# Scoring one head group in whole fp32 on small array tiles, in a two-layer attention encoder on one Trainium2 core

## The chip, the cores and the metric

The kernel runs on one core of a Trainium2 chip. A core has five engines that run side by side and meet at semaphores: TensorE (PE: matrix products, with its weight loads shown as PEld), VectorE (DVE), ScalarE (ACT), GpSimd (POOL) and SyncE (SP, which issues the transfers). Products land in PSUM, in eight banks of 512 fp32 columns; everything else that is computed on lies in SBUF, with 128 partitions. The metric is the time of one execution on the device in microseconds (us), as the median of several runs.

## The reference

The model is an encoder block of two layers on 512 tokens of width 1024, with 16 heads of 64. The change touches layer A, whose mixer has three groups of heads that differ in dilation (1, 4 and 16), each with its own queries, keys and values; the groups are merged by their softmax denominators.

```python
def mixer_a(hn, w_in, w_out, q_gain, k_gain, t5_bias):
    proj = hn @ w_in
    ...
    for g, (window, dilation) in enumerate(DILATED_PAIRS):     # (128,1), (512,4), (2048,16)
        q = rms_norm(qkv[:, :, g, 0], q_gain[g])
        k = rms_norm(qkv[:, :, g, 1], k_gain[g])
        v = qkv[:, :, g, 2]
        reach = (window // 2) // dilation
        o, lse = dilated_group_attention(q, k, v, t5_bias[...], dilation, reach)
    ...
    alpha = jax.nn.softmax(jnp.stack(lses), axis=0)
    y = jnp.sum(alpha[..., None] * jnp.stack(outs), axis=0)
    y = y.reshape(b, s, BRANCH_WIDTH).astype(hn.dtype) * jax.nn.silu(gate)
    return y @ w_out
```

Each query of group 0 sees the 64 tokens on either side; the logits are q.k/8 plus a bias by distance, all in float32. Layer B is a neighbourhood attention on an 8 x 64 grid, built alike: norm, one projection, per-head norm of queries and keys, softmax, gate, output projection.

## The kernel before

**Tiles and passes.** The 16 heads go through as eight pairs (`hc` 0 to 7), each pair filling 128 partitions, one head in the lower 64 and one in the upper. For most products float32 values are split in two halves, a rounded high part `h` and the rest `l`, both of type fp32r, and a product is made of three: h.h, h.l and l.h (`mm3`, L221). Weights come in by SyncE into `wraw`, ScalarE rounds them to `wh` (L132), and VectorE or GpSimd subtracts to give `wl` (L138). The projections are the bulk of TensorE's work (tile `acc`).

**Order of the work.** TensorE's order is written out by hand. A main generator yields after each group of projection products; a side generator makes the attention, and `run` (L932) lets the side go on whenever a clock of the kernel's own (`clock`, L209, advanced by an estimate of each product in `matmul`, L211) passes the time at which the side's next piece is due. The due times are delays in ns of that clock after stamps such as `("rawk", hc + 1)`. The other engines' instructions are ordered when the program is built, some of them pinned by `keep_in_program_order`.

**Queries and keys of layer A.** Of each pair the projection gives `rawq` with four column blocks of 128: queries of groups 0, 1 and 2, and keys of group 0. For pairs 0 to 5 (`moved`, L446) VectorE transposes 32x32 blocks in place (L571), and the tile goes to DRAM and back (`move_q`, L609: one write, four reads) into `qt`, which has four slots: slots 0 to 2 the queries of groups 0 to 2, slot 3 the keys of group 0, now with a head's 64 dimensions on the partitions. For pairs 6 and 7, `q_a` (L587) transposes on TensorE instead (`transpose4`) and copies out of PSUM. Group 0's queries and keys are then split: `split_q` (L639) or `q_a` fill `q0h`, `q0l`, `k0h`, `k0l`, with the product of the query and key gains (`gk`) folded into one of the two by `put_k` (L658). The keys of groups 1 and 2 lie in `k12` in plain float32, transposed and scaled in `k_a` (L560).

**Scores.** `scores(u)` in `attn_a` (L789, L797) makes the logits of two tiles of 128 queries, t = 2u and 2u+1, for both heads, each tile and head in a PSUM bank `log`: columns 0 to 255 for group 0 (a window of 192 or 256 keys), columns 256 to 511 for the dilated groups. Group 0 goes first for both tiles, by `mm3_heads` (L226): three split products for each head, of 64 rows (the head's dimensions) by 128 columns (queries) of the array, the two heads in its two halves. Then come groups 1 and 2: for each group g, each j of 4 slices of 32 queries and each head, one product in plain float32 on an array tile of 64 rows by 32 columns:

```python
matmul(
    lgs[hd][32 * j : 32 * j + 32, 256 + P * g : 384 + P * g],
    qt[hs, t, 1 + g, 32 * j : 32 * j + 32],
    k12[hs, g, P * j : P * j + P],
    share=2, start=False, stop=(g == 1),
)
```

So slice j meets keys 128j to 128j+127 of its own residue class. VectorE adds the bias and finds the minimum of the negated logits (L835, L846), ScalarE takes the exponential (L857), and later `weigh` makes the weighted sums `o`.

**Layer B.** `side_b` (L1050) splits its queries and keys in the same way into tiles `qh`, `ql`, `kh`, `kl`, which use the same four buffers (the tags `q0h`, `q0l`, `k0h`, `k0l`), and scores with `mm3_heads`.

Of the kernel before, what the change touches and what calls it, by code (L numbers as in the profile page):

```python
# [22 lines left out]
P = 128  # L23
S = 512
# [7 lines left out]
EXT = S + 64  # L32
# [14 lines left out]
def tile_hybrid_encoder(  # L47
# [12 lines left out]
    nc = tc.nc  # L60
# [5 lines left out]
    wk = ctx.enter_context(tc.tile_pool(name="wk", bufs=2))  # L66
# [19 lines left out]
    def bank(name):  # L86

        return ps_side.tile([P, 512], F32, tag="side", name=name)
# [122 lines left out]
    def matmul(o, l, r, share=1, **kw):  # L211

        cols = max(r.free_size() / 2.4, l.free_size() / 1.2)
        clock[0] += (cols if r.dtype == F32R else r.free_size() * 4 / 2.4 * l.free_size() / P) / share
        nc.tensor.matmul(o, l, r, **kw)  # L215
# [166 lines left out]
    gk = cp.tile([P, 4], F32, name="gk")  # L382
# [59 lines left out]
    st = {}  # L442
# [133 lines left out]
    def q_tiles():  # L576


        return (
            wk.tile([P, 512], F32R, tag="q0h", name="q0h", bufs=1),  # L580
            wk.tile([P, 512], F32R, tag="q0l", name="q0l", bufs=1),
            wk.tile([P, 4, 4, P], F32, tag="q12", name="qt", bufs=1),
            wk.tile([P, EXT], F32R, tag="k0h", name="k0h", bufs=1),
            wk.tile([P, EXT], F32R, tag="k0l", name="k0l", bufs=1),
        )

    def q_a(hc):  # L587

        yield "wait", ("rawq", hc), 18000 if moved(hc) else 13000 if hc < NHC - 1 else 23500
        raw = st.pop(("rawq", hc))  # L590
        if moved(hc):
            move_q(hc, raw)
            return
        st["q", hc] = q0h, q0l, qt, k0h, k0l = q_tiles()

        tp = transpose4(raw, 0)
        nc.scalar.copy(tjr(q0h), to_tjr(tp))
        nc.vector.tensor_sub(tjr(q0l), to_tjr(tp), tjr(q0h.bitcast(F32)))
        yield
        tp = transpose4(raw, 3 * P)  # L600
        put_k([(trj(k0h[:, 64:EXT]), trj(k0l[:, 64:EXT]), to_trj(tp))], 0)
        yield
        for g in range(2):
            tp = transpose4(raw, (g + 1) * P)
            nc.vector.tensor_copy(qt[:, :, 1 + g, :].rearrange("p t (j r) -> p t j r", j=4), to_tjr(tp))
            yield
        stamp["q", hc] = 0

    def move_q(hc, raw):  # L609

        d = dr.tile([4, P, 512], F32, name="qd", tag="qd", bufs=2)
        tiles = q_tiles()
        qt, left = tiles[2], [4]
# [24 lines left out]

    def split_q(q0h, q0l, qt, k0h, k0l):  # L639
        src = qt[:, :, 3, :].rearrange("p t (j r) -> p t r j", j=4)  # L640
        trj4 = lambda t: t[:, 64:EXT].rearrange("p (t r j) -> p t r j", t=4, j=4)
        tc.keep_in_program_order(nc.scalar.copy(trj4(k0h), src))
        by_t = lambda t: t.rearrange("p (t x) -> p t x", t=4)
        put_k([(by_t(q0h), by_t(q0l), qt[:, :, 0, :])], 0, True)
        nc.vector.tensor_sub(trj4(k0l), src, trj4(k0h.bitcast(F32)))

    def v_a(hc):

# [6 lines left out]
        stamp["v", hc] = 0  # L655
        yield

    def put_k(parts, g, pinned=False):  # L658

        for dh, _, src in parts:  # L660
            m = nc.scalar.activation(dh, src, AF.Copy, scale=gk[:, g : g + 1])
            if pinned:
                tc.keep_in_program_order(m)
        for dh, dl, src in parts:
            nc.vector.scalar_tensor_tensor(
                dl, src, gk[:, g : g + 1], dh.bitcast(F32), op0=ALU.mult, op1=ALU.subtract
            )

    def side_by_side(o, mms, first=True):

# [117 lines left out]

    def attn_a(hc):  # L789
        e0, e12 = st.pop(("e", hc))  # L790
        q0h, q0l, qt, k0h, k0l = st.pop(("q", hc))
        k12, v12 = st.pop(("k12", hc))
        pts, turners = [pq], []

# [2 lines left out]
        def scores(u):  # L797

            tiles = []
            for t in (2 * u, 2 * u + 1):  # L800
                cs, n = (64, 192) if t == 0 else (0, 192) if t == 3 else (0, 256)
                tiles.append((t, [bank("log") for _ in range(2)], cs, n))
            for t, lgs, cs, n in tiles:
                ks = slice(P * t + cs, P * t + cs + n)
                qs = slice(P * t, P * t + P)
                mm3_heads(
                    [lg[:, cs : cs + n] for lg in lgs],
                    lambda hs: q0h[hs, qs], lambda hs: q0l[hs, qs],
                    lambda hs: k0h[hs, ks], lambda hs: k0l[hs, ks], False,
                )  # L810
            for t, lgs, cs, n in tiles:
                for g in range(2):
                    for j in range(4):
                        for hd in range(2):
                            hs = slice(64 * hd, 64 * hd + 64)
                            matmul(
                                lgs[hd][32 * j : 32 * j + 32, 256 + P * g : 384 + P * g],
                                qt[hs, t, 1 + g, 32 * j : 32 * j + 32],
                                k12[hs, g, P * j : P * j + P],
                                share=2,  # L820
                                start=False,
                                stop=(g == 1),
                            )
# [87 lines left out]
        else:  # L911
            for u in range(2):
                if u == 0:
                    yield "wait", ("gate", hc), 500
                yield 600
                held = scores(u)
                yield 3200
                if pending:
                    yield "wait", ("gate", hc - 1), 16800
                    pending.pop(0)()  # L920
                    yield
                for args in held:
                    turn_p(*args)
                    yield
# [125 lines left out]
    def side_b(hc):  # L1050
# [7 lines left out]
        yield "wait", ("raw", hc), (12000, 33000, 12000, 26000, 17500, 33500, 11000, 26000)[hc]  # L1058
        raw = st.pop(("raw", hc))
        e = st.pop(("e", hc))  # L1060
        qh = wk.tile([P, 512], F32R, tag="q0h", name="qh", bufs=1)
        ql = wk.tile([P, 512], F32R, tag="q0l", name="ql", bufs=1)
        kh = wk.tile([P, EXT], F32R, tag="k0h", name="kh", bufs=1)[:, :S]
        kl = wk.tile([P, EXT], F32R, tag="k0l", name="kl", bufs=1)[:, :S]
        tp = transpose4(raw, 0)
        for src, dst in ((mid_rc(tp), mid_q(qh)), (edge_rc(tp), edge_q(qh))):
            nc.scalar.copy(dst, src)
# [4 lines left out]
            nc.vector.tensor_sub(l, src, h.bitcast(F32))  # L1072
        yield 2500 if hc < NHC - 1 else 2000
        tp = transpose4(raw, P)
        put_k([(kh, kl, tp)], 3)
        stamp["qk", hc] = 0
        yield 1750 if hc < NHC - 1 else 1250
        pt, turners = pq[:, 2048 * (hc % 2) : 2048 * (hc % 2) + 2048], []
# [117 lines left out]
    def side():  # L1196
# [48 lines left out]
        for hc in range(NHC):  # L1245
            yield from side_b(hc)
# [100 lines left out]
```

## Time and profile before

| | |
|---|---|
| median of 3 runs | 845.8 us (845.26 to 847.01) |
| span of the profiled execution | 843.7 us, 14965 instructions |
| granted TensorE clock, whole span | 1.000 |
| split and float32 score products of layer A | 93.1 to 533.5 us of the span |
| DMA | 141.20 MB, mean 167 GB/s |
| HBM | read 109.11 MB, written 31.12 MB |

The profile is one execution; its times are us from the first instruction, and its span is the time from the first to the last instruction. A group of instructions is named by the line that issues it, the engine, the operation and "out<-in" by the names of the tiles. All products have line L215, the helper's, so they are told apart by their tiles; a shape such as 64*32 64x192 means that the product holds 64 rows by 32 columns of the array and streams 192 columns. Products are pipelined: the end of one overlaps the next, so the distance of two starts tells more than a length. TensorE's weight loads run beside its products.

### The profile page before, as it was taken

How to read it: one execution, taken by the hardware profiler on the slowest of the kernel's cores; microseconds unless marked ns; L12 is line 12 of the kernel's file. 1: busy time of each engine (PE TensorE's matmuls, PEld its weight loads, DVE VectorE, ACT ScalarE, POOL GpSimd, SP SyncE). 2: the span in 40 equal slices, each digit the busy share in tenths (PEclk: the TensorE clock that was granted, in tenths of full speed). 3: DMA queues.
4: the chain of work that ended last, by engine and by line, in shares of the span. 5: the costliest groups of instructions: out<-in, count | busy, mean ns of one | idle time of the engine just before them, and what ended most of it. 6: DMA issues, size and time to landing. Idle time of an engine off the chain costs nothing.

```text
span 843.7 us, 14965 instructions
## 1 busy us (share of the span) xinstructions
PE 837.7 (99%) x5378; PEld 676.3 (80%) x5378; DVE 528.4 (63%) x1371; ACT 427.8 (51%) x899; POOL 294.2 (35%) x432
## 2 busy tenths in 40 slices
PE   9999999999999999999999999999999999999998
PEld 7788888788788788788788787888878877777777
DVE  7354684684674674675674675447565777668653
ACT  7432653563553653652653564344366465664541
POOL 3352442452441541542532341121521625235211
PEclk9999999999999999999999999999999999999999
DMA  6345478378378278378276364164236546447323
GB/s 253 112 132 178 150 215 248 139 212 259 124 213 258 98 227 246 95 235 244 92 220 189 115 195 110 60 233 176 78 102 197 155 145 191 121 150 202 102 92 131
DMA packets 64218, 141.20 MB, mean 167 GB/s; under 512 B 5648, under 2 KB 23248, under 8 KB 64144
## 3 DMA queue, kind: packets, MB, share of 16 engines
q1 hardware_dynamic: 64000, 139.99, 54.0%
q8 instruction: 42, 0.69, 0.3%
q10 hardware_dynamic: 144, 0.26, 0.1%
q14 instruction: 32, 0.26, 0.1%
HBM read 109.11 MB, written 31.12 MB: 166 GB/s over the span
## 4 chain that ended last, share of the span: by engine, by line
PE 95%; DMA 2%; ACT 1%; DVE 1%; issue 0%; SPq 0%; ACTq 0%
PE acc L215 80%; PE log L215 5%; PE o L215 5%; PE tp L219 3%; DMA pt<-td 1%; DMA wraw<-in_w 1%; DVE hn_l L403 1%; ACT p L1119 1%; DMA x_all<-in_xt 0%; ACT p L694 0%; DVE pt L1017 0%; PE pa L215 0%; ACT raw L485 0%; PE pl L215 0%; PE pk L215 0%
## 5 line engine op out<-in xcount | busy, mean ns | idle before, releaser
L132 ACT CAST wh<-wraw 128x512 fp32r<-128x512 f32 (+1 forms) x259 | 158.3, 612 | 283.5 <-PE acc L215 246.0
L215 PE MATMUL acc<-wh,hn_h 128*128 128x512 f32 x704 | 282.4, 402 | 1.1 <-ACT hn_h L402 0.7
L215 PE MATMUL acc<-wh,hn_l 128*128 128x512 f32 x704 | 274.2, 390 | 0.0
L215 PE MATMUL acc<-wl,hn_h 128*128 128x512 f32 x704 | 274.1, 390 | 0.0
L138 POOL TENSOR_TENSOR wl<-wraw,wh 128x512 fp32r<-128x512 f32 (+1 forms) x104 | 135.2, 1300 | 366.1 <-ACT wh L132 344.5
L138 DVE TENSOR_TENSOR wl<-wraw,wh 128x512 fp32r<-128x512 f32 (+1 forms) x156 | 111.8, 717 | 146.4 <-ACT wh L132 145.3
L215 PEld LDWEIGHTS acc<-wh,hn_h 128*128 128x128 f32 x704 | 132.1, 188 | 35.8 <-issue 5.6
L215 PEld LDWEIGHTS acc<-wh,hn_l 128*128 128x128 f32 x704 | 132.2, 188 | 28.6
L215 PEld LDWEIGHTS acc<-wl,hn_h 128*128 128x128 f32 x704 | 132.4, 188 | 25.2 <-POOL wl L138 0.3
L215 PE MATMUL acc<-y,wh 128*128 128x512 f32 (+1 forms) x272 | 82.5, 387 | 0.0
L215 PE MATMUL acc<-hn_h,wh 128*128 128x512 f32 x192 | 76.1, 396 | 0.0
L215 PE MATMUL acc<-hn_h,wl 128*128 128x512 f32 x192 | 74.9, 390 | 0.0
L215 PE MATMUL acc<-hn_l,wh 128*128 128x512 f32 x192 | 74.8, 389 | 0.0
L694 ACT ACTIVATE p<-p,mn 128x512 f32<-128x512 f32 (+3 forms) x128 | 69.4, 585 | 0.6 <-DVE mn L693 0.2
L857 ACT ACTIVATE p<-p,mn 128x512 f32<-128x512 f32 (+1 forms) x64 | 44.8, 701 | 46.8 <-DVE mn L846 46.5
L291 DVE TENSOR_REDUCE ss<-sq 128x4 f32<-128x256 f32 (+1 forms) x96 | 48.3, 505 | 30.1 <-POOL sq L290 18.7
L770 DVE STREAM_TRANSPOSE tr<-p 128x512 f32<-128x512 f32 (+1 forms) x80 | 53.7, 683 | 12.3 <-ACT p L694 11.6
L215 PEld LDWEIGHTS acc<-y,wh 128*128 128x128 f32 x272 | 48.1, 189 | 9.6 <-issue 1.3
L215 PE MATMUL acc<-y,wl 128*128 128x512 f32 (+1 forms) x136 | 51.4, 378 | 0.0
L215 PEld LDWEIGHTS acc<-hn_h,wh 128*128 128x128 f32 x192 | 36.1, 188 | 8.0 <-issue 0.3
L215 PEld LDWEIGHTS acc<-hn_h,wl 128*128 128x128 f32 x192 | 36.0, 188 | 7.7
L215 PEld LDWEIGHTS acc<-hn_l,wh 128*128 128x128 f32 x192 | 36.1, 188 | 7.0
(143 smaller groups left out, 1041.1 us busy)
## 6 DMA issues: line engine op xcount, KB each, us to landing
wraw<-in_w SPq DMA_DIRECT2D x119, 512.0 KB
td<-tr SPq DMA_DIRECT2D x14, 1024.0 KB
pt<-td SPq DMA_DIRECT2D x56, 256.0 KB
qd<-rawq SPq DMA_DIRECT2D x6, 1024.0 KB
qt<-qd SPq DMA_DIRECT2D x24, 256.0 KB
td<-tr SPq DMA_DIRECT2D x6, 896.0 KB
pt<-td SPq DMA_DIRECT2D x24, 224.0 KB
e<-l_d SPq DMA_DIRECT2D x32, 112.0 KB
```

Of the source, the lines that this page charges most:

```text
L132: nc.scalar.copy(h, raw)
L138: eng.tensor_sub(l, raw, h.bitcast(F32))
L215: nc.tensor.matmul(o, l, r, **kw)
L219: nc.tensor.transpose(o, i, ident)
L291: nc.vector.tensor_reduce(ss[:, i * ns : (i + 1) * ns], sq.rearrange("p (a b) -> p a b", b=64), axis=AX.X, op=ALU.add)
L403: return nc.vector.scalar_tensor_tensor(l, xk, g, h.bitcast(F32), op0=ALU.mult, op1=ALU.subtract)
L694: nc.scalar.activation(pr, pr, AF.Copy, scale=mn[:, 3:4])
L770: nc.vector.transpose(dst, src[:, :n].rearrange("p (i b k) -> p i b k", b=4, k=32))
L857: nc.scalar.activation(row, row, AF.Exp, bias=mn[:, 1:2], scale=-1.0, accum_out=mn[:, 2:3])
L1119: nc.scalar.activation(pr[:, o : o + n], pr[:, o : o + n], AF.Exp, bias=mn[:, 0:1], scale=-1.0, accum_out=mn[:, 2:3])
```

## The change

Group 0 of layer A is scored like the dilated groups: one float32 product for each slice of 32 queries and each head, on array tiles of 64 rows by 32 columns, over the window's 192 or 256 keys. Its queries are read from slot 0 of `qt`; its keys are scaled once into `k0`, in float32. The tiles `q0h`, `q0l`, `k0h`, `k0l` are gone, and so are the instructions that filled them. `put_k` becomes `scaled`, a single ScalarE activation. The products now run tile by tile, with group 0 first and then groups 1 and 2 of the same tile; the first product into a slice's quarter of a bank has `start` set. In pairs 6 and 7, group 0's queries are copied into slot 0 of `qt`. Layer B keeps its split; its four tiles become quarters of one tile that uses the buffer of `qt`.

```diff
@@ q_tiles
         return (
-            wk.tile([P, 512], F32R, tag="q0h", name="q0h", bufs=1),
-            wk.tile([P, 512], F32R, tag="q0l", name="q0l", bufs=1),
             wk.tile([P, 4, 4, P], F32, tag="q12", name="qt", bufs=1),
-            wk.tile([P, EXT], F32R, tag="k0h", name="k0h", bufs=1),
-            wk.tile([P, EXT], F32R, tag="k0l", name="k0l", bufs=1),
+            wk.tile([P, EXT], F32, tag="k0", name="k0", bufs=1),
         )
@@ q_a
         tp = transpose4(raw, 0)
-        nc.scalar.copy(tjr(q0h), to_tjr(tp))
-        nc.vector.tensor_sub(tjr(q0l), to_tjr(tp), tjr(q0h.bitcast(F32)))
+        nc.scalar.copy(qt[:, :, 0, :].rearrange("p t (j r) -> p t j r", j=4), to_tjr(tp))
         yield
         tp = transpose4(raw, 3 * P)
-        put_k([(trj(k0h[:, 64:EXT]), trj(k0l[:, 64:EXT]), to_trj(tp))], 0)
+        scaled(trj(k0[:, 64:EXT]), to_trj(tp), 0)
@@
-    def split_q(q0h, q0l, qt, k0h, k0l):
+    def split_q(qt, k0):
         src = qt[:, :, 3, :].rearrange("p t (j r) -> p t r j", j=4)
-        trj4 = lambda t: t[:, 64:EXT].rearrange("p (t r j) -> p t r j", t=4, j=4)
-        tc.keep_in_program_order(nc.scalar.copy(trj4(k0h), src))
-        by_t = lambda t: t.rearrange("p (t x) -> p t x", t=4)
-        put_k([(by_t(q0h), by_t(q0l), qt[:, :, 0, :])], 0, True)
-        nc.vector.tensor_sub(trj4(k0l), src, trj4(k0h.bitcast(F32)))
+        dst = k0[:, 64:EXT].rearrange("p (t r j) -> p t r j", t=4, j=4)
+        tc.keep_in_program_order(scaled(dst, src, 0))
@@
-    def put_k(parts, g, pinned=False):
...
+    def scaled(dst, src, g):
+        return nc.scalar.activation(dst, src, AF.Copy, scale=gk[:, g : g + 1])
@@ attn_a, scores
             for t, lgs, cs, n in tiles:
                 ks = slice(P * t + cs, P * t + cs + n)
-                qs = slice(P * t, P * t + P)
-                mm3_heads(
-                    [lg[:, cs : cs + n] for lg in lgs],
-                    lambda hs: q0h[hs, qs], lambda hs: q0l[hs, qs],
-                    lambda hs: k0h[hs, ks], lambda hs: k0l[hs, ks], False,
-                )
-            for t, lgs, cs, n in tiles:
-                for g in range(2):
-                    for j in range(4):
-                        for hd in range(2):
-                            hs = slice(64 * hd, 64 * hd + 64)
-                            matmul(
-                                lgs[hd][32 * j : 32 * j + 32, 256 + P * g : 384 + P * g],
-                                qt[hs, t, 1 + g, 32 * j : 32 * j + 32],
-                                k12[hs, g, P * j : P * j + P],
-                                share=2,
-                                start=False,
-                                stop=(g == 1),
-                            )
+                parts = [(0, j, slice(cs, cs + n), k0, ks) for j in range(4)] + [
+                    (1 + g, j, slice(256 + P * g, 384 + P * g), k12[:, g, :], slice(P * j, P * j + P))
+                    for g in range(2)
+                    for j in range(4)
+                ]
+                for g, j, cols, keys, of in parts:
+                    for hd in range(2):
+                        hs = slice(64 * hd, 64 * hd + 64)
+                        matmul(
+                            lgs[hd][32 * j : 32 * j + 32, cols],
+                            qt[hs, t, g, 32 * j : 32 * j + 32],
+                            keys[hs, of],
+                            share=2,
+                            start=(g == 0),
+                            stop=(g == 2),
+                        )
@@ side_b
-        qh = wk.tile([P, 512], F32R, tag="q0h", name="qh", bufs=1)
-        ql = wk.tile([P, 512], F32R, tag="q0l", name="ql", bufs=1)
-        kh = wk.tile([P, EXT], F32R, tag="k0h", name="kh", bufs=1)[:, :S]
-        kl = wk.tile([P, EXT], F32R, tag="k0l", name="kl", bufs=1)[:, :S]
+        qk = wk.tile([P, 4, S], F32R, tag="q12", name="qkb", bufs=1)
+        qh, ql, kh, kl = (qk[:, i, :] for i in range(4))
...
-        put_k([(kh, kl, tp)], 3)
+        scaled(kh, tp, 3)
+        nc.vector.scalar_tensor_tensor(kl, tp, gk[:, 3:4], kh.bitcast(F32), op0=ALU.mult, op1=ALU.subtract)
```

More of the change, by code (lines that the diff above doesn't have):

```diff
@@ L593, in q_a @@
             return
-        st["q", hc] = q0h, q0l, qt, k0h, k0l = q_tiles()
+        st["q", hc] = qt, k0 = q_tiles()
         tp = transpose4(raw, 0)
-        nc.scalar.copy(tjr(q0h), to_tjr(tp))
-        nc.vector.tensor_sub(tjr(q0l), to_tjr(tp), tjr(q0h.bitcast(F32)))
+        nc.scalar.copy(qt[:, :, 0, :].rearrange("p t (j r) -> p t j r", j=4), to_tjr(tp))
         yield
         tp = transpose4(raw, 3 * P)
-        put_k([(trj(k0h[:, 64:EXT]), trj(k0l[:, 64:EXT]), to_trj(tp))], 0)
+        scaled(trj(k0[:, 64:EXT]), to_trj(tp), 0)
         yield
@@ L612, in move_q @@
         tiles = q_tiles()
-        qt, left = tiles[2], [4]
+        qt, left = tiles[0], [4]
         def write():
@@ L656, in v_a @@
         yield
-    def put_k(parts, g, pinned=False):
[L660 to L666, printed above, removed]
-            )
+    def scaled(dst, src, g):
+        return nc.scalar.activation(dst, src, AF.Copy, scale=gk[:, g : g + 1])
     def side_by_side(o, mms, first=True):
@@ L790, in attn_a @@
         e0, e12 = st.pop(("e", hc))
-        q0h, q0l, qt, k0h, k0l = st.pop(("q", hc))
+        qt, k0 = st.pop(("q", hc))
         k12, v12 = st.pop(("k12", hc))
@@ L804, in scores @@
                 ks = slice(P * t + cs, P * t + cs + n)
-                qs = slice(P * t, P * t + P)
-                mm3_heads(
-                    [lg[:, cs : cs + n] for lg in lgs],
-                    lambda hs: q0h[hs, qs], lambda hs: q0l[hs, qs],
-                    lambda hs: k0h[hs, ks], lambda hs: k0l[hs, ks], False,
-                )
-            for t, lgs, cs, n in tiles:
-                for g in range(2):
-                    for j in range(4):
-                        for hd in range(2):
-                            hs = slice(64 * hd, 64 * hd + 64)
-                            matmul(
-                                lgs[hd][32 * j : 32 * j + 32, 256 + P * g : 384 + P * g],
-                                qt[hs, t, 1 + g, 32 * j : 32 * j + 32],
-                                k12[hs, g, P * j : P * j + P],
-                                share=2,
-                                start=False,
-                                stop=(g == 1),
-                            )
+                parts = [(0, j, slice(cs, cs + n), k0, ks) for j in range(4)] + [
[14 more added lines that the diff above has]
+                        )
             return [
```

## The prediction

> **What bounds the kernel now.** I read the page first, then the waits of TensorE alone, then the sums by stretch, and last TensorE's timeline around the scores that the change rewrites. From the page, the busy shares, the granted clock and the chain that ended last:
>
> ```profile
> span 843.7 us, 14965 instructions
> PE 837.7 (99%) x5378; PEld 676.3 (80%) x5378; DVE 528.4 (63%) x1371; ACT 427.8 (51%) x899; POOL 294.2 (35%) x432
> PEclk9999999999999999999999999999999999999999
> PE acc L215 80%; PE log L215 5%; PE o L215 5%; PE tp L219 3%; DMA pt<-td 1%; DMA wraw<-in_w 1%; DVE hn_l L403 1%; ACT p L1119 1%; DMA x_all<-in_xt 0%; ACT p L694 0%; DVE pt L1017 0%; PE pa L215 0%; ACT raw L485 0%; PE pl L215 0%; PE pk L215 0%
> ```
>
> TensorE (PE) is busy for 99% of the span at full clock, and the projections (acc) are 80% of the chain, the scores (log) of both layers 5%. A busy share alone doesn't show that nothing is waited for, so the waits of TensorE come next, with total us, times and the longest:
>
> ```profile
> PE busy L377 <- DVE warm L366: 0.9, 1, 0.9
> PE o L215 <- DMA pt<-td: 0.8, 1, 0.8
> PE acc L215 <- ACT hn_h L402: 0.7, 1, 0.7
> PE acc L215 <- ACT raw L485: 0.3, 1, 0.3
> PE acc L215 <- DVE pt L1017: 0.2, 1, 0.2
> ```
>
> That is 2.9 us in all. The sums by stretch show that none of it lies where layer A makes its scores (stretch, length, busy us and instructions of each engine, clock, DMA share, GB/s):
>
> ```profile
> 60.00:548.00 488.00, 487.99 (x3532) 396.75 (x3532) 308.62 (x775) 243.14 (x472) 178.94 (x262) 1.00 0.59 179
> ```
>
> TensorE idles 0.01 us of 488. In this stretch the time is the length of TensorE's own stream: work taken from ScalarE (ACT) and VectorE (DVE) is worth nothing by itself, and what is added to or taken from the stream counts in full.
>
> One score unit covers two query tiles and both heads of a pair; there are 16, two for each of 8 pairs. Here are the two units of the first pair in TensorE's timeline (start, length of the merged row):
>
> ```profile
> 92.59 0.39 PE L215 MATMUL acc<-wl,hn_h 128*128 128x512 f32 x1
> 92.81 0.39 PE L215 MATMUL acc<-wh,hn_l 128*128 128x512 f32 x1
> 93.13 0.36 PE L215 MATMUL log<-k0h,q0h 64*128 64x192 f32 x2
> 93.33 0.28 PE L215 MATMUL log<-k0l,q0h 64*128 64x192 f32 x2
> 93.44 0.28 PE L215 MATMUL log<-k0h,q0l 64*128 64x192 f32 x2
> 93.55 0.30 PE L215 MATMUL log<-k0h,q0h 64*128 64x256 f32 x2
> 93.69 0.28 PE L215 MATMUL log<-k0l,q0h 64*128 64x256 f32 x2
> 93.81 0.28 PE L215 MATMUL log<-k0h,q0l 64*128 64x256 f32 x2
> 94.02 1.18 PE L215 MATMUL log<-k,qt 64*32 64x128 f32 x64
> 95.13 0.50 PE L215 MATMUL acc<-wh,hn_h 128*128 128x512 f32 x1
> ...
> 102.83 0.39 PE L215 MATMUL log<-k0h,q0h 64*128 64x256 f32 x2
> ...
> 103.70 1.18 PE L215 MATMUL log<-k,qt 64*32 64x128 f32 x64
> 104.81 0.50 PE L215 MATMUL acc<-wh,hn_h 128*128 128x512 f32 x1
> ```
>
> Starts are what counts, since ends overlap. In the first unit the 12 split products of group 0 hold the stream from 93.13 to 94.02, 0.89 us; the dilated groups hold it from 94.02 to 95.13, 1.11 us, in 64 pieces. The second unit, which takes its tiles the other way round, has 0.87 and 1.11. A unit is 2.00 or 1.98 us, 1.99 on the mean.
>
> **The change, part by part: TensorE.** Gone from each unit are the 12 split products and the step from 64*128 to 64*32, 0.88 us on the mean. In their place stand 2 tiles x 4 slices of 32 queries x 2 heads = 16 fp32 products, 8 over 192 keys and 8 over 256. The dilated groups' 2 x 2 x 4 x 2 = 32 products are 64 pieces in the trace, so a product is two pieces and group 0 adds 32 of them (16 and 16). What a piece costs I read from the dilated groups of the first unit, by asking the timeline for windows that end ever later; the length of each row is that of the pieces begun so far:
>
> ```profile
> 94.02 0.34 PE L215 MATMUL log<-k,qt 64*32 64x128 f32 x8
> 94.02 0.45 PE L215 MATMUL log<-k,qt 64*32 64x128 f32 x16
> 94.02 0.56 PE L215 MATMUL log<-k,qt 64*32 64x128 f32 x24
> 94.02 0.67 PE L215 MATMUL log<-k,qt 64*32 64x128 f32 x32
> 94.02 0.83 PE L215 MATMUL log<-k,qt 64*32 64x128 f32 x40
> 94.02 1.18 PE L215 MATMUL log<-k,qt 64*32 64x128 f32 x64
> ```
>
> Eight pieces, one for each of the 8 tiles of 64*32 in the array, take 0.11 us for 128 columns: the eight run side by side. (The step from x32 to x40 is 0.16, and the last 24 take 0.35, 0.12 for eight: a little is lost at the second query tile.) No row shows a 64*32 piece of another width. The nearest are the weighing products on 128*64, two side by side:
>
> ```profile
> 149.31 1.97 PE L215 MATMUL o<-pt,rawk 128*64 128x128 f32 x32
> 151.10 1.90 PE L215 MATMUL o<-pt,v 128*64 128x256 f32 x16
> 152.93 0.50 PE L215 MATMUL acc<-wh,hn_h 128*128 128x512 f32 x1
> ```
>
> Pairs of 128 columns take 1.79 / 16 = 0.112 us, pairs of 256 take 1.83 / 8 = 0.229 with the step back to 128*128 in it: an fp32 piece costs by its columns. So eight pieces of 192 columns should take 0.11 x 1.5 = 0.165 and eight of 256 0.22, and group 0 takes 2 x 0.165 + 2 x 0.22 = 0.77 us. A new unit is 1.11 + 0.77 = 1.88 us against 1.99, **0.11 us less**; the 0.32 us from the last projection product (92.81) to the unit's first (93.13) stays, since a step from 128*128 to a smaller tile stays. 16 x 0.11 = **1.8 us less**.
>
> Both ends of that: if the loss at the second query tile (0.05 at x40, 0.02 in the rest) goes, because wider pieces let the supply catch up, each unit gains another 0.07, 2.9 us less in all. If start, loss and hand-over are not paid once but grow with the columns, the 1.11 us scale as a whole: 1.11 x (32 x 224) / (64 x 128) = 0.97 for group 0, a unit of 2.08, and 16 x 0.09 = 1.4 us more. I stay near the cadence rows, which are the same engine, tile shape and keys layout.
>
> **Vector side.** From the views of the split tiles (ns minimum, median, maximum), what prepared q0 and k0, in pairs 0 to 5 from the moved tile and in 6 and 7 from a transpose:
>
> ```profile
> L642 ACT CAST k0h<-qt x6: 1116/1183/1223, 88.5 to 405.2; 128x512 fp32r<-128x512 f32 x6
> L661 ACT ACTIVATE q0h<-qt,gk x6: 730/773/782, 89.5 to 406.3; 128x512 fp32r<-128x512 f32 x6
> L645 DVE TENSOR_TENSOR k0l<-qt,k0h x6: 1070/1082/1126, 89.7 to 406.4; 128x512 fp32r<-128x512 f32 x6
> L665 DVE SCALAR_TENSOR_TENSOR q0l<-qt,gk,q0h x6: 735/748/762, 90.7 to 407.4; 128x512 fp32r<-128x512 f32 x6
> L598 DVE TENSOR_TENSOR q0l<-tp,q0h x2: 653/672/692, 450.2 to 494.2; 128x512 fp32r<-128x512 f32 x2
> L665 DVE SCALAR_TENSOR_TENSOR k0l<-tp,gk,k0h x2: 742/746/749, 452.1 to 495.9; 128x512 fp32r<-128x512 f32 x2
> ```
>
> VectorE loses 6 x (1.08 + 0.75) + 2 x (0.67 + 0.75) = 13.8 us, ScalarE 6 x 0.77 = 4.6 us; the one write of k0 that stays takes about the 1.18 of the cast with the same pattern. Against the 0.01 us of idle TensorE in this stretch I cost all of it at nothing. It also moves k0 and q0 away from the path: today the last of the four ends at 90.7 + 0.75 = 91.5, 1.6 us ahead of the unit at 93.13; afterwards TensorE needs one write that starts where k0h does, at 88.5, and ends near 89.7. That cover of 3.4 us would have to go before the write cost anything. No transfer is added, removed or reordered: q0 and k0 already came with qt, whose four slots were read anyway. PSUM tiles are as many as before, and tile t's scores are now whole before tile t+1's begin, so VectorE's minimum (L835) on the first tile can start earlier.
>
> In layer B the four split tiles become one of 4 x 512 columns. The same four writes fill it and the same score products read all four, so it comes free when they did; those scores wait for nothing in the list of waits above. Were ScalarE's kh write held for VectorE's ql, it would lie inside the 2500 ns (L1073) between the two transposes. I cost it at nothing.
>
> The kernel's own clock (L211) books group 0 at 8 x 53.3 + 8 x 40 = 747 ns a unit instead of 12 x 106.7 / 2 = 640, 107 ns more. Side work that follows can come at most one step of three projection products earlier; that changes the order of the stream, not its length.
>
> **The sum.** Against the profiled execution: 843.7 - 1.8 = 841.9 us of span. The median of the runs, 845.8, is 2.1 us above that span, and I leave those as they are: **844.0 us**.
>
> **The rivals.** What this kernel's runs can tell from no change is about 0.2%, 1.7 us, so the forecast itself lies just at that edge.
>
> (a) The overheads grow with the pieces, as in the upper bound above: +1.4, 847.2 us. For it: the 0.16 step at x40 is unexplained. Against: x8 to x32 keep 0.11.
>
> (b) The pieces are limited by how fast they can be started, not by columns. The slowest eight above took 0.16 us, 0.02 each; 96 such pieces are 1.92 us, still 0.07 under 1.99, so 844.7 us, and only a start rate worse than any row shows makes it slower. The Trainium skill (TensorE: Matmul & The Clock Gate, Part 1) says that start to start never falls below about 25 ns however few columns a product has; by that rule 96 pieces need an estimated 2.4 us, the unit is 0.41 longer and the kernel ends near 852.4. The trace disagrees: 64 pieces in 1.11 us are 17 ns each, 8 in 0.11 are 14.
>
> (c) **Slower, by one mechanism**: the four slices of 32 queries now stream the same key columns of k0 at once, while each of today's reads its own 128 columns of k12. If such reads of one address queue up behind each other, group 0's 0.77 becomes up to four times as long: 2.31 more per unit, 37 us in all less the 1.8, 881 us. It decides from 0.11 / 0.77, 14% more on these pieces. For it: no row shows shared columns on several column tiles. Against: today's four slices already read the same 64 partitions side by side at full cadence.
>
> (d) The other engines' queues come out in another order, and TensorE finds a wait in layer A. The longest wait behind the start-up is 0.8 (the o products for pt<-td); one such in each of 8 pairs is 6.4, less 1.8: 850.4 us. Against: the work only shrinks, and 308.62 of 488 us leave VectorE room.
>
> (e) The freed engines also remove waits: of the 2.9 us, 1.6 lie in the start-up (0.9 and 0.7) which the change doesn't reach; the other 1.3 us would give 842.7.
>
> **How the numbers follow.** Forecast 0.54 (its own range 842.9 to 845.0, the two bounds with most of the upper one left to (a)); (a) 0.15; (b) 0.05; (c) 0.06; (d) 0.10; (e) 0.10. The range runs from 842.3, the forecast with the loss gone and some of (e), to 847.2, (a); it leaves out (c), (d) and the tails. Faster by over 1.7 us is below 844.1: some 70% of the forecast (its centre lies 0.1 us below, and the gain can still grow by the recovered loss, while most of what shrinks it is counted in (a)), and (e): 0.48. Slower by over 1.7 us, above 847.5: (c), (d) and a third of (a): 0.21. Within: 0.31.
>
> **What would show it.** The row log<-k,qt on 64*32 becomes x96 a unit with k0 in it, with forms of 192 and 256 columns; TensorE counts 5378 - 12 x 16 + 32 x 16 = 5698. From the last projection product before a unit to the first behind it should be 2.2 us where it is 95.13 - 92.81 = 2.32 now. Eight pieces of 256 columns that take 0.22 fit the forecast; clearly more is (c). VectorE's busy time falls by about 14 us without worth. A wait of TensorE between 60 and 548 us would be (d). The prediction is wrong if units stay at 1.99 or more, or if TensorE's waits change by more than 1 us.

## The result, and the profile after

The changed kernel takes 844.52 us (median of 11 runs, 843.16 to 845.30) against 845.53 (11 runs, 845.07 to 847.01); the ratio is 0.9978, with a 95% interval of 0.9970 to 0.9986. The forecast was 844.0, in a range of 842.3 to 847.2. The two profiled executions differ by more than the medians, 843.7 to 841.7 us of span, 2.0 us; more on these two figures stands below, under the warm-up. The gain of the medians, 1.0 us, is a little over half of the 1.8 us that were forecast.

From the page after, the span and the busy shares; TensorE has the 5698 instructions that were counted out, VectorE lost 12.6 us and ScalarE 2.5:

```profile
span 841.7 us, 15565 instructions
PE 836.5 (99%) x5698; PEld 675.6 (80%) x5698; DVE 515.8 (61%) x1355; ACT 425.3 (51%) x893; POOL 284.8 (34%) x432
```

The waits of TensorE (total us, times, longest) are 2.0 us now:

```profile
PE busy L377 <- DVE warm L366: 0.9, 1, 0.9
PE acc L215 <- ACT hn_h L402: 0.4, 1, 0.4
PE acc L215 <- ACT raw L485: 0.3, 1, 0.3
PE log L215 <- DVE qkb L1056: 0.2, 1, 0.2
PE acc L215 <- DVE pt L999: 0.2, 1, 0.2
```

The 0.8 us for pt<-td is gone, a wait of the scores of layer B for qkb has come. In the stretch with layer A's scores nothing has changed but the work (columns as before):

```profile
60.00:548.00 488.00, 488.00 (x3863) 396.97 (x3862) 297.07 (x763) 241.66 (x469) 169.46 (x262) 1.00 0.60 179
```

TensorE is busy without a gap, and now starts 331 more instructions in the same 488 us. Here are the first pair's two units in TensorE's timeline, as they were shown before; the row's form is that of its first piece:

```profile
93.12 0.39 PE L215 MATMUL acc<-wh,hn_l 128*128 128x512 f32 x1
93.44 1.91 PE L215 MATMUL log<-k,qt 64*32 64x192 f32 x96
95.28 0.50 PE L215 MATMUL acc<-wh,hn_h 128*128 128x512 f32 x1
...
102.67 0.39 PE L215 MATMUL acc<-wh,hn_l 128*128 128x512 f32 x1
102.98 1.99 PE L215 MATMUL log<-k,qt 64*32 64x256 f32 x96
104.90 0.50 PE L215 MATMUL acc<-wh,hn_h 128*128 128x512 f32 x1
```

The reader is to see three things. The step from the last projection product to the unit's first piece is 0.32 us as before (93.12 to 93.44). The first unit lasts 1.84 us (93.44 to 95.28) where it was 2.00. The second lasts 1.92 (102.98 to 104.90) where it was 1.98. This pattern holds through the kernel: the eight first units are 1.84, the second units 1.92 in pairs 0 to 5 and 1.84 in pairs 6 and 7.

Where the 2.0 us between the two profiled executions come from, by the distance of starts on TensorE:

| place | before, us | after, us | in all, us |
|---|---|---|---|
| first units of the 8 pairs | 2.00 | 1.84 | -1.2 |
| second units, pairs 0 to 5 | 1.98 | 1.92 | -0.3 |
| second units, pairs 6 and 7 | 1.98 | 1.84 | -0.3 |
| transposes at 508 us | 0.28 and 0.09 | 0.11 and 0.03 | -0.2 |
| ahead of the o products at 766 us | 1.14 | 0.38 | -0.8 |
| score unit of layer B at 775 us | 0.91 | 1.37 | +0.5 |
| first dozen products | | | +0.3 |

The score units give 1.8 us less, and the other rows together 0.2 us less.

### The profile page after: what moved, and what is told of

Same layout as the page of the kernel before. It is cut to its first block, busy times and chain, and to the rows that moved or that the text cites. A ratio compares the mean times of both kernels' runs of the same rounds, so it can differ in the third digit from the quotient of the medians.

```text
span 841.7 us, 15565 instructions
## 1 busy us (share of the span) xinstructions
PE 836.5 (99%) x5698; PEld 675.6 (80%) x5698; DVE 515.8 (61%) x1355; ACT 425.3 (51%) x893; POOL 284.8 (34%) x432
## 4 chain that ended last, share of the span: by engine, by line
PE 96%; DVE 1%; ACT 1%; DMA 0%; issue 0%; ACTq 0%
PE acc L215 82%; PE log L215 5%; PE o L215 5%; PE tp L219 3%; DVE hn_l L403 1%; DMA x_all<-in_xt 0%; ACT p L1100 0%; ACT p L679 0%; DVE pt L999 0%; PE pa L215 0%; ACT raw L485 0%; PE pl L215 0%; PE pk L215 0%; DVE qkb L1056 0%; DVE qkb L1052 0%
## 5 line engine op out<-in xcount | busy, mean ns | idle before, releaser
L138 DVE TENSOR_TENSOR wl<-wraw,wh 128x512 fp32r<-128x512 f32 (+1 forms) x156 | 114.5, 735 | 148.8 <-ACT wh L132 148.2
```

Of the source, the lines that this page charges most:

```text
L138: eng.tensor_sub(l, raw, h.bitcast(F32))
```

## The experiments

Five questions were open: what group 0 costs in either form, what the gain consists of, why six units are slower than the rest, whether vector side and layer B count for anything, and why single runs spread more than the change is worth.

**Group 0 twice.** In the changed kernel the products of group 0 are issued twice, the second time over the first:

```diff
-                for g, j, cols, keys, of in parts:
+                for n, (g, j, cols, keys, of) in enumerate(parts[:4] + parts):
...
-                            stop=(g == 2),
+                            stop=(n < 4 or g == 2),
```

> Group 0's products issued twice, the second time over the first (same output). If eight pieces cost by their columns at the cadence 0.165 (192) and 0.22 us (256), each unit grows by 2 x 0.165 + 2 x 0.22 = 0.77 us and the kernel by 16 x 0.77 = 12.3 us. If start and hand-over grew with the pieces (rival a) it would be 0.97 a unit, 15.5 us; if shared key columns queued up (rival c), more than 0.88 a unit, over 14 us.

Measured: 856.6 us (median of 4 runs, 854.71 to 857.87); the span is 853.9, 12.2 above the changed kernel's. The first unit in TensorE's timeline:

```profile
93.39 2.67 PE L215 MATMUL log<-k,qt 64*32 64x192 f32 x128
95.98 0.50 PE L215 MATMUL acc<-wh,hn_h 128*128 128x512 f32 x1
```

93.39 to 95.98 is 2.59 us with 128 pieces where 96 took 1.84: group 0 costs 0.75 us a unit (0.756 by the unrounded starts, the same in all 16). The cadence stated 0.77. Neither the scaled overheads of rival (a), 0.97, nor queued reads of shared keys, rival (c), are there. The span grew by 16 x 0.756 = 12.1 us and 0.1 more.

**The kernel before with group 0 twice.** The split products doubled in the same way:

```diff
-                mm3_heads(..., False)
+                for again in (True, False):
+                    mm3_heads(..., again)
```

> The kernel before with group 0's split products issued twice, the second time over the first (same output). This prices the streaming of the split products without the change of tile shape around them. Theory: three fp32r products of 64*128 start 0.11 us apart per pair of heads, so 6 x 0.11 = 0.66 to 0.68 us a unit, 10.8 us in all, which is less than the 0.756 us that whole fp32 on 64*32 measured when doubled; the gain of the change is then not in the products but in the shape switch that is gone (0.88 less 0.67, 0.2 us a unit). Rival: the split products themselves cost their whole 0.88 us a unit, 14 us in all.

Measured: 858.31 us (median of 4 runs, 857.92 to 858.45). The first unit:

```profile
94.69 0.36 PE L215 MATMUL log<-k0h,q0h 64*128 64x192 f32 x2
...
95.10 0.27 PE L215 MATMUL log<-k0h,q0h 64*128 64x192 f32 x2
...
96.28 1.18 PE L215 MATMUL log<-k,qt 64*32 64x128 f32 x64
97.39 0.50 PE L215 MATMUL acc<-wh,hn_h 128*128 128x512 f32 x1
```

94.69 to 97.39 is 2.70 us, 0.70 more than 2.00. Split and doubled, group 0 costs less than whole fp32, 0.70 against 0.756, though each unit of the changed kernel is shorter. (The span grew by 12.5 us, 1.3 more than 16 x 0.70: most of that because this execution began slowly, as described under the warm-up.) So the change loses 0.06 us a unit on the products, and wins 0.88 - 0.70 = 0.18 on what stood around them: the first pair of the new shape (0.20 us to the next pair, 93.13 to 93.33 in the profile before, where later pairs take 0.11) and the step to 64*32 behind the last (0.21 us from 93.81 to 94.02, where the pair before took 0.12).

**The shape brought back.** If the step is the gain, whole fp32 on 64*128 must lose it. Group 0 by one product for each head, for both tiles first, then the dilated groups:

```diff
+                if first:
+                    for hd in range(2):
+                        hs = slice(64 * hd, 64 * hd + 64)
+                        matmul(lgs[hd][:, cs : cs + n], qt[hs, t, 0, :], k0[hs, ks], share=2, start=True, stop=False)
+                    continue
```

> Group 0 in whole fp32, but on 64*128 (all 128 queries of a tile in one product for each head), for both tiles first, then the dilated groups on 64*32 as in group0_first; this brings the shape switch inside the unit back. Doubling gave 0.756 us a unit for whole fp32 on 64*32 and 0.70 for the split products, and the split products held 0.88 in all, so the switch with what it delays is about 0.18 us. Theory (the gain is the switch that is gone): a unit takes 1.868 + 0.18 = 2.05 us, more than the 1.99 of the kernel before, and the kernel ends about 1 us above the kernel before in its units. Rival (whole fp32 gains by itself, whatever the tile): the unit stays near 1.87.

Measured: 845.91 us, ratio to the kernel before 1.0003 (0.9992 to 1.0013). The first unit, and the same stretch asked for in windows that end earlier:

```profile
93.14 2.14 PE L215 MATMUL log<-k,qt 64*128 64x192 f32 x72
95.20 0.50 PE L215 MATMUL acc<-wh,hn_h 128*128 128x512 f32 x1
```

```profile
93.14 0.43 PE L215 MATMUL log<-k,qt 64*128 64x192 f32 x2
93.14 0.60 PE L215 MATMUL log<-k,qt 64*128 64x192 f32 x4
93.14 0.81 PE L215 MATMUL log<-k,qt 64*128 64x192 f32 x6
93.14 1.03 PE L215 MATMUL log<-k,qt 64*128 64x192 f32 x8
```

2.06 us (2.069 in all 16 units), 0.20 above the same order on 64*32 in the next experiment. The streaming is not what differs: by the starts in the trace of the first unit, a pair of pieces of 192 columns takes 0.16 us here and one of 256 takes 0.215, so two of each come to the same 0.756. The 0.20 are the first pair of the new shape (0.27 us to the next pair instead of 0.16) and the step to 64*32 behind the last (0.31 instead of 0.215), 0.10 each. So that the fp32 products need no splitting is worth nothing in time by itself; the gain comes from their sharing the array shape with the dilated groups.

**Group 0 first for both tiles.** The changed kernel goes tile by tile. Here group 0 of both tiles comes first, as before the change:

```diff
-            for t, lgs, cs, n in tiles:
+            for first, (t, lgs, cs, n) in [(f, x) for f in (True, False) for x in tiles]:
...
-                for g, j, cols, keys, of in parts:
+                for g, j, cols, keys, of in parts[:4] if first else parts[4:]:
```

> Products of group 0 for both tiles first, then the dilated groups of both, as in the kernel before; everything else as changed. Of the changed kernel's units 10 take 1.84 us from first product to the next projection product and 6 (the second units of pairs 0 to 5) take 1.92, where two waits of TensorE's sequencer and a late third piece stand in the middle, at the second tile. Theory: these are the waits for the second tile's banks, and asked for early in the unit they are met without cost; the 6 units fall to about 1.84 and the span by 6 x 0.08 = 0.5 us. Rival: the wait is for the banks themselves, which come free late whatever the order; then the 6 units stay at 1.92 or more. By either the other 10 units stay at 1.84.

Measured: 842.85 us (7 runs, 842.59 to 844.89), ratio to the kernel before 0.9963 (0.9950 to 0.9976). All 16 units take 1.868 us:

```profile
93.07 1.94 PE L215 MATMUL log<-k,qt 64*32 64x192 f32 x96
94.94 0.50 PE L215 MATMUL acc<-wh,hn_h 128*128 128x512 f32 x1
```

Half of the theory holds. The six units fell from 1.92 to 1.87, but not to 1.84, and the other ten rose from 1.84 to 1.87, which neither theory had; the sum is the same to 0.1 us. That the waits are those of the second tile is seen in the view of line 215 for single units of the changed kernel. The second unit of pair 1 has two waiting instructions in TensorE's sequencer, and that of pair 6, which takes 1.84 us, has no such row:

```profile
L215 PEld LDWEIGHTS log<-k,qt x96: 102/106/108, 166.2 to 167.8; 64*32 64x32 f32 x96
L215 PE MATMUL log<-k,qt x96: 268/269/401, 166.2 to 167.9; 64*32 64x128 f32 x64, 64*32 64x256 f32 x16, 64*32 64x192 f32 x16
L215 PEldq EVENT_SEMAPHORE  x2: 51/51/51, 166.9 to 167.1; - x2
```

They start at 166.9 and 167.1, at the second tile's first pieces. In the order by groups the same unit has them at its start:

```profile
L215 PEldq EVENT_SEMAPHORE  x2: 51/51/51, 165.8 to 166.0; - x2
```

There the units with the two waits take 1.868 us like those without: asked for early, they cost nothing that can be seen. The 0.025 us that the other units lose lie at their end. From the first piece of the last eight to the next projection product it is 0.32 us in this order, as in the kernel before, and 0.30 in the ten short units of the changed kernel. In this order the unit ends with 64 pieces of 128 columns in a row, in the changed kernel with 32; that this is the reason was not tried.

**Vector-side work put back.** Work of about the same size as what was removed runs again, onto a tile that nobody reads. Shown is the edit for pairs 0 to 5; pairs 6 and 7 get two such VectorE operations each:

```diff
         tc.keep_in_program_order(scaled(dst, src, 0))
+        again = wk.tile([P, 512], F32R, tag="again", name="again", bufs=1)
+        tc.keep_in_program_order(scaled(again.rearrange("p (t x) -> p t x", t=4), qt[:, :, 0, :], 0))
+        nc.vector.tensor_sub(again.rearrange("p (t r j) -> p t r j", t=4, j=4), src, dst)
+        nc.vector.scalar_tensor_tensor(
+            again.rearrange("p (t x) -> p t x", t=4), qt[:, :, 0, :], gk[:, 0:1], qt[:, :, 0, :],
+            op0=ALU.mult, op1=ALU.subtract,
+        )
```

> The changed kernel with the removed vector-side work put back on a tile that nobody reads: per moved pair one ScalarE activation (0.77 us) and two VectorE operations (1.08 and 0.75), per other pair two VectorE operations of about 0.7. VectorE's busy time goes back to about 529 us, ScalarE's to about 430. Theory: worth nothing, the median stays within 0.5 us of the changed kernel's. Rival: the gain of the change lies in the vector side; then the time goes back by 1 to 2 us, to 845.5.

Measured: 844.81 us (843.19 to 847.03, 12 runs) against the changed kernel's 844.52; the ratio to the kernel before is 0.9978 (0.9967 to 0.9988), that of the changed kernel 0.9978. The busy shares are back, from its page:

```profile
PE 837.8 (99%) x5698; PEld 676.8 (80%) x5698; DVE 530.9 (63%) x1371; ACT 429.2 (51%) x899; POOL 291.7 (35%) x432
```

VectorE has 15.1 us more than in the changed kernel, and the score units are as long, 1.84 and 1.92, with a sum of 30.0 us in both. The vector side is worth nothing in the units, and nothing in the time as far as an interval of 0.2% can tell.

**Four tiles in layer B.** Layer A as changed, layer B's split queries and keys in four tiles again:

```diff
-        qk = wk.tile([P, 4, S], F32R, tag="q12", name="qkb", bufs=1)
-        qh, ql, kh, kl = (qk[:, i, :] for i in range(4))
+        qh = wk.tile([P, EXT], F32R, tag="k0", name="qh", bufs=1)[:, :S]
+        ql, kh, kl = (wk.tile([P, S], F32R, tag=n, name=n, bufs=1) for n in ("ql", "kh", "kl"))
```

> Layer A as changed, layer B's split queries and keys in four tiles again (one of them in the buffer of k0). The 2.0 us that the span lost come from layer A's score units (measured sum 1.84 us) and layer B only trades one wait for another (the o products' 0.76 us for pt<-td is gone, 0.46 us for DVE qkb before one score unit has come). Theory: the one tile does not cause that new wait, it is there because TensorE arrives earlier; then this run equals the changed kernel within 0.3 us in the units of both layers, and a wait of about 0.4 us before the log unit near 772 us is still there. Rival: the one tile holds writers back; then that wait is gone and the span is about 0.4 us below the changed kernel's 841.7.

Measured: 843.22 us (7 runs, 842.98 to 845.12), ratio 0.9968 (0.9954 to 0.9982). Its profiled execution began slowly (see the warm-up), so its span of 843.1 us can't be held against the changed kernel's 841.7, and the units have to tell. The 16 score units of layer A have the same sum, 30.0 us. The wait is still there, now by the name kl; the first rows are of the changed kernel, the second of this one:

```profile
772.68 0.38 PE L215 MATMUL log<-qkb 64*128 64x256 f32 x2
773.25 0.86 PE L215 MATMUL log<-qkb 64*128 64x256 f32 x10 [0.19 <-DVE qkb L1056]
```

```profile
774.07 0.38 PE L215 MATMUL log<-kh,qh 64*128 64x256 f32 x2
774.62 0.38 PE L215 MATMUL log<-kl,qh 64*128 64x256 f32 x2 [0.17 <-DVE kl L1056]
```

In both, the second pair starts 0.55 to 0.57 us behind the first instead of 0.22, and the unit takes 1.37 and 1.33 us instead of 0.91. So the one tile isn't its cause. With the vector work back, where TensorE waits 0.5 us for pt<-td ahead of it, this unit takes 0.91 as in the kernel before: of the two waits the one that comes first takes the other's place, in part.

**The warm-up.** Single runs spread by more than the change is worth, and the profiles show where. These are the products in flight in two-us stretches at the start (columns: stretch, length, TensorE's busy us and instructions, clock, DMA share, GB/s), in the changed kernel and in four_tiles_b:

```profile
6.00:8.00 2.00, 2.00 (x10) 1.00 1.02 417
8.00:10.00 2.00, 2.00 (x10) 1.00 1.04 426
```

```profile
6.00:8.00 2.00, 2.00 (x6) 1.00 1.02 412
8.00:10.00 2.00, 2.00 (x7) 1.00 1.02 416
```

Both read a clock of 1.00, yet one has 10 products in flight where the other has 6. By the starts they lie 0.23 us apart in the one and 0.43 in the other, for nine products from 6.2 to 9.9 us, 1.6 us lost. The first execution took 843.49 us, the second 844.84. The Trainium skill (TensorE: Matmul & The Clock Gate, Part 1) has TensorE's clock halved after an idle window of about 3.4 us and freed after a busy one, the windows running freely; 0.43 is what it gives for 512 columns at half rate, and the trace agrees with the length, but its clock column doesn't show it. By that rule a pause of 0.4 to 0.95 us, as TensorE has it ahead of the first projection product in the profiles here, is too short to halve the clock. The next runs fill the pause ahead of the first projection product:

```diff
-    for _ in range(8):
+    for _ in range(11):
         wide = lambda n: ones[:, 0:1].to_broadcast([P, n])
         nc.tensor.matmul(busy, wide(P), wide(S), start=True, stop=True)
```

> The kernel before with 11 instead of 8 warm-up products (tile busy, L376). In the profiles so far the first dozen projection products start 0.23 us apart in some executions and 0.43 apart in others, until about 10 us, and the times of every kernel fall into two groups about 1.6 us apart (the changed kernel: 843.2 to 843.5 and 844.5 to 845.3). Theory: the spread is TensorE running its first window at half rate after the pause between the last warm-up product (4.07 us) and the first projection product (5.1 to 5.6); with the pause filled, the upper group goes and the times lie near 845.3, spread under 1 us. Rival: the half-rate window comes whatever fills the pause; then two groups stay.

> The changed kernel with 11 warm-up products, to compare with the kernel before under the same start. By the score units alone the change is worth 1.84 us (10 units of 1.84 instead of 2.00 or 1.98, 6 of 1.92), so about 843.4 if the other lands at 845.3. If the change were worth only the 1.0 us that lies between the two medians (845.53 and 844.52), 844.3.

> Group 0's products first for both tiles, and 11 warm-up products. Its units were 1.868 us, all 16, against 10 of 1.843 and 6 of 1.920: the same sum to 0.1 us. So by the units it equals the changed kernel with the long warm-up within 0.3 us; what the 842.85 us of the shorter warm-up had beyond that (0.46 us of a wait before a score unit of layer B) may come or go.

And with 13:

> The kernel before with 13 warm-up products. With 11, all its 11 runs lay between 845.3 and 846.2, where 8 gave a second group at 846.6 to 848. Theory (the pause ahead of the first projection product brings the half-rate window): one group again, near 845.5. Rival: chance; values above 846.5 come back.

> The changed kernel with 13 warm-up products. With 11, the products reached full rate early, ended at 4.9 us and left a pause of 0.55 us, and times went from 842.95 to 845.34. Theory: with the pause filled the times draw together near 843.3, spread under 1 us, and the change is worth about 2 us (0.24%) against before_warmup_13. Rival: the spread stays, so it has another cause too.

| warm-up products | before, us | changed, us |
|---|---|---|
| 8 | 845.53 (845.07 to 847.01) | 844.52 (843.16 to 845.30) |
| 11 | 845.45 (845.27 to 846.19) | 843.81 (842.95 to 845.34) |
| 13 | 846.16 (845.41 to 846.82) | 843.49 (843.01 to 843.84) |

The second and third rows are from two different chips. On these, the kernel before with 8 products took 845.88 us (844.98 to 847.93, 23 runs) and 846.21 (845.10 to 847.83, 21 runs); the changed kernel with 8 was not run there.

With group 0 first and 11 warm-up products: 843.84 us (842.58 to 844.59), the same as the changed kernel with 11, as its units foretold, although its profiled execution has a wait inside layer A that no other profile has: 0.9 us at 319.6 us for ScalarE's copy gt (L533). With 11, one group was left in the kernel before, but not in the changed one, whose warm-up ended early in its profile and left TensorE idle for 0.4 us (4.70 to 5.46 from start to start). With 13 the changed kernel's five runs lie within 0.8 us; the kernel before has one of 11 runs above 846.5, which the theory had not allowed. So the slow start is shown as one cause of the spread, worth 1.6 us. It is not shown to be the only one.

What sets the slow start off is only in part shown. The idle time ahead of the first projection product was 0.49, 0.60 and 0.65 us in the three profiles that began slowly (four tiles in layer B, the kernel before with group 0 twice, the vector-side work put back). It was 0.39 to 0.95 us in the six others that have a pause (in the changed kernel's only the first two gaps are long). So the length of the pause doesn't decide. The warm-up products at first start 0.43 us apart in every profile. The change to 0.23 comes between 4.0 and 6.6 us in most, and between 8.6 and 10.4 us in those three; in the five profiles without a pause it is never late. That fits the theory, but five are few. Filling the pause also has a price: in the profile of mixed order, below, all 13 warm-up products keep to 0.43, and the first projection product starts at 6.63 us, where it was 5.1 to 5.6 with 8.

What it means for the change: with 8 products the times fall into two groups, and 8 of 11 runs of the kernel before are in the lower one but 4 of 11 of the changed kernel. The lower groups lie 2.1 us apart (medians 845.4 and 843.3) and the upper ones 1.9 (847.0 and 845.15). So the 1.0 us between the medians most likely compares a different mix of starts, and the 1.8 us by the units, or the 2.0 us of the two profiled executions, are nearer to what the change does; one execution of each kernel was profiled, so the mix itself is not shown. With 11 and 13 products the medians differ by 1.6 and 2.7 us. With 13 the ratios to the kernel before with 8 are 0.9993 (0.9985 to 1.0002) and 0.9962 (0.9948 to 0.9975).

**Mixed order.** Group 0 first only in the second units of pairs 0 to 5, tile by tile elsewhere, with 13 warm-up products:

```diff
+            early = moved(hc) and u == 1
+            for first, (t, lgs, cs, n) in [(f, x) for f in ((True, False) if early else (True,)) for x in tiles]:
...
+                for g, j, cols, keys, of in (parts[:4] if first else parts[4:]) if early else parts:
```

> The changed kernel with 13 warm-up products and the order by groups in the second units of pairs 0 to 5 alone, which took 1.92 us tile by tile and 1.868 with group 0 first; the others stay tile by tile at 1.843. By the units 6 x 0.05 = 0.3 us less than after_warmup_13. If the order by groups slows a unit for another reason than those waits, nothing.

Measured: 842.87 us (842.77 to 843.76), ratio 0.9959 (0.9947 to 0.9972). The six units take 1.868 and the ten 1.842, as foretold; the 0.3 us are too little for the times, whose intervals overlap with those of after_warmup_13. It has the lowest sum of units of all versions and beats the kernel before; that it beats the changed kernel with the same warm-up is shown by its units alone.

## Why the prediction was right

- **What bounds the stretch.** The prediction rested on the 0.01 us that TensorE idled between 60 and 548 us. It idles none there after the change either, and the vector work put back left the sum of the units as it was. Right.
- **The cost of group 0 in whole fp32**, read from the dilated groups' cadence and scaled by columns: 0.77 us a unit, measured 0.756. Right.
- **The cost of what goes**, 0.88 us by starts: right as a sum, since the step between shapes was counted in. What the prediction did not say is that this step is more than the gain: products alone, the change loses 0.06 us a unit.
- **The unit**: 1.88 on the mean forecast, 1.87 measured, but as 10 units of 1.84 and 6 of 1.92. That the long ones meet two waits at the second query tile was not foreseen. The short ones are shorter than forecast, but not by the loss at x40 that the favourable bound went by. By the starts there is no such loss: in the kernel before, each eight from the third on begins 0.109 us after the one ahead of it, at x40 too, and the longer row only shows that the last pieces of an eight start later. What the short ones gain is 0.01 us on group 0 and 0.03 at the end of the unit. The two departures nearly cancel; that the mean came out so close is partly luck.
- **VectorE, ScalarE, the one tile in layer B**: each costed at nothing, and nothing was found. ScalarE lost 2.5 us of busy time where 4.6 were forecast; its write of k0 takes 1.29 us, not 1.18. The claim that layer B's scores wait for nothing was true of the kernel before alone: with the pt<-td wait gone, one unit came ahead of its keys and took 0.46 us longer.
- **The kernel's clock**: transposes in pairs 1 to 5 moved one step of three projection products forward, as bounded, without a change in length that can be seen.
- **The sum**: 841.9 us of span forecast, 841.7 measured. The median was 0.5 above the forecast, most likely for the start-up and not for the change. The waits of TensorE fell by 0.9 us, just inside the 1 us that was named as a sign of being wrong.
- **The rivals**: (a) needed 0.97 us for group 0 and (c) more than 0.88, against 0.756; (b) needed starts 20 ns apart, where the 8 first pieces start within 0.05 us; its 1.92 us are what six units take, but these have the two waits, and the ten without take 1.84. The 25 ns of the Trainium skill (TensorE: Matmul & The Clock Gate, Part 1) hold for no unit, 96 pieces in 1.84 us being 19 ns each. (d) found no wait in layer A in the changed kernel; the one of 0.9 us with group 0 first and 11 warm-up products is of its kind. (e) came in part: 0.8 us of waits went, 0.5 came.

## What to carry to other kernels

Where one engine runs without a gap, price an edit by distances of starts on that engine, and count the step between array shapes as part of a group of products: here it was three times as large as the difference between split and whole fp32, and of the other sign. Double a group of products to get its cost without its surroundings; what is left of its share in the timeline is the surroundings. Before trusting a gain of 0.2%, look at whether two executions began alike.

## What was not expected of the hardware

- Pieces on 64*32 start 7 ns apart on different tiles of the array, and sharing key columns four ways slows nothing: doubling added 0.756 us, which is 2 x 0.162 + 2 x 0.216, where the unshared 0.109 for 128 columns gives 0.164 and 0.218 by columns.
- The step from 64*128 to 64*32, with the first pair's delay in the new shape, costs 0.18 to 0.20 us, over a quarter of what the twelve split products of a unit cost when doubled (0.70).
- TensorE can start its first ten or so projection products 0.43 us apart instead of 0.23 while the clock column of the profile reads 1.00.
- Two waits of 51 ns in the middle of a burst of small pieces are not hidden: the six units that have them are 0.08 us longer than the units without. At the start of a unit two such waits cost nothing that can be seen (1.868 us with and without). That the waits alone make up the 0.08 was not isolated, since moving them ahead changed the order of the pieces as well.
